# Seven block products in place of eight in a down projection on one core

## The chip, the cores and the metric

The kernel runs on one NeuronCore of a Trainium2 chip. The core has five engines with instruction queues of their own: TensorE (PE in the profile; its weight loads are shown apart as PEld), VectorE (DVE), ScalarE (ACT), GpSimd (POOL) and SyncE (SP, which only issues transfers here). The metric is the device time of one execution in microseconds (us); lower is better. PSUM, which TensorE writes its products to, has eight banks; one bank holds a tile of 128 x 512 float32.

## The reference

One layer of a post-norm encoder on a sequence of 512 tokens and 1024 channels: a token mixer of three branches, then a gated MLP with a causal convolution. Only the MLP's end matters here. With `h` (512 x 1024) after the second modulation and `c` the condition:

```python
def _conv_ffn(h, w_up, conv_w, conv_b, w_down):
    z = h @ w_up                                # 512 x 5632
    ...                                         # three-tap causal convolution along the sequence
    val, gate = jnp.split(zc, 2, axis=-1)
    return (jax.nn.silu(gate) * val) @ w_down   # 512 x 2816 times 2816 x 1024

    y = _conv_ffn(h, w_up[l], conv_w[l], conv_b[l], w_down[l])
    x = _layer_norm(ALPHA * x + gt_f[:, None, :] * y) * ln_f_g[l] + ln_f_b[l]
```

`gt_f` is a row of 1024 gates, a matrix product of `silu(c)` with a slice of `w_ada`, plus a bias.

## The kernel before, in words

Every large product is computed in three matmuls: an operand is split into a high part (rounded to the fast matmul type) and a low part (the remainder), and high x low, low x high and high x high are added up in one PSUM bank. The split of a weight tile is a cast on ScalarE (high) and a subtraction on VectorE (low).

The layer runs as one straight program; TensorE goes from one product to the next: input projections and attention, the pooling branch and its merge, the gating branch (`uv_half`, `gated`) and the other two merges, an output projection (`project_out` with name "o"), the up projection, and the down projection (`project_out` with name "d").

A framework orders the instructions of each engine beforehand from the program's dependencies: where a step of higher rank (earlier in the program) isn't ready, a later one that is ready can be put ahead of it. `behind_split(work)` puts a piece of side work behind the latest subtraction of a weight split on the same engine. Tiles of one tag share a fixed number of buffers: `raw` (128 x 1024, three; weights as loaded), `whi` and `wlo` (two each; split weights of the moment), `act` (48 of 128 x 512), `h` (16), `pt` (8), `pad` (5). A load on SP waits until a buffer of its tag is free, and what is queued behind it on SP waits with it.

**Up projection** (the loop `for i in range(NP)`, NP = 22). A turn makes two 128-row blocks of `z` (one of the values, one of the gates, 24 matmuls each), the convolution (L1410, L1413, L1417), the SiLU (L1427) and the product on GpSimd (L1428). The result, channels x tokens, is split into `f{i}h` and `f{i}l` (L1431, L1432). On every second turn up to the 16th it also loads and adds up one piece of `w_ada` for the gates (`ada_piece`); after the last of them `ada_rows` sums over partitions with four matmuls against ones (`pgt`, L871) and leaves the gate row, broadcast to 128 partitions, in `gtfb`.

**Down projection** (L1124 to L1158, then `mm3` at L107 to L109). It has 22 chunks k of 128 rows of `w_down`. Each chunk is loaded (512 KB), **multiplied by the gate row on GpSimd** (L1124, two halves), split, and multiplied with the four token tiles t and two column halves n: 4 x 2 x 3 matmuls of 512 columns into eight banks, which are all in use from the first chunk to the last. The first 18 chunks pass through `whi`/`wlo`; the last four are split into resident tiles of tag `h` (L1134, L1135), so that the last products can be ordered by output: all four chunks of one (t, n), then the next. After each t, `finish` adds the residual straight from PSUM (L1448), takes the statistics (L1455, L1457), and normalises and stores the 128 rows: two centrings on VectorE (L1462), one half scaled on VectorE (L1474), the other on ScalarE (L1471) and GpSimd (L1472). The last half of the last tile is computed in two products of 256 columns, so that its statistics come sooner (L1454).

## Time and profile before

| | before |
|---|---|
| median of three runs | 953.91 us (953.81 to 954.74) |
| profiled execution, own time | 953.8 us |
| its span, first to last instruction | 952.1 us |
| outside the span | 1.7 us |
| granted TensorE clock | 0.998 |

The profile's page gives the busy time of each engine, the span in 40 slices, the transfer queues, the chain of work that ended last, and the costliest groups of instructions. Other views of the trace give that chain or all instructions in order of time, groups of instructions by line and shape, busy times by stretch, and the instructions around one tile. Durations are in us; "mean ns of one" in nanoseconds; "idle before, releaser" is how long the engine stood still ahead of an instruction and who ended that.

### The profile page before, as it was taken

The numbers are of one execution on the slowest core, as the hardware profiler recorded it, in microseconds if no ns is written. First come the engines' busy times: TensorE is split into PE (matmuls) and PEld (weight loads), VectorE is DVE, ScalarE is ACT, GpSimd is POOL, SyncE is SP. The second block draws the span as 40 slices with busy tenths as digits, with TensorE's granted clock in tenths as the row PEclk, the third lists the DMA queues.
The fourth block names the chain that finished last, engine by engine and source line by source line (L and its number), as shares of the span: only waits on it lengthen the run. The fifth ranks groups of instructions, "written<-read, shape, count | busy, mean of one in ns | idle before, by whom it ended". The sixth has DMA issues, their size and how long they took to land.

```text
span 952.1 us, 12075 instructions
## 1 busy us (share of the span) xinstructions
PE 938.9 (99%) x4524; PEld 792.6 (83%) x4524; DVE 594.2 (62%) x860; ACT 380.5 (40%) x623; POOL 290.7 (31%) x258
## 2 busy tenths in 40 slices
PE   7999999999999999999999999999999999999996
PEld 6988888888888888888888889988888888888885
DVE  7966668546686575667244589575655665733268
ACT  4576555533334322233322434654444444321121
POOL 4741121122350032303053713021111121756653
PEclk9999999999999999999999999999999999999999
DMA  9823212144436533554244440233343342432222
GB/s 323 323 64 109 59 34 83 45 133 154 133 100 215 194 112 121 177 190 154 90 134 131 156 155 24 68 126 117 112 135 129 116 127 90 127 116 89 97 81 88
DMA packets 46458, 119.77 MB, mean 126 GB/s; under 512 B 5792, under 2 KB 9280, under 8 KB 46400
## 3 DMA queue, kind: packets, MB, share of 16 engines
q1 hardware_dynamic: 45648, 118.39, 38.0%
q8 instruction: 35, 0.57, 0.2%
q10 hardware_dynamic: 432, 0.55, 0.2%
q14 instruction: 23, 0.19, 0.1%
q0 software_dynamic: 320, 0.07, 0.0%
HBM read 116.86 MB, written 2.13 MB: 125 GB/s over the span
## 4 chain that ended last, share of the span: by engine, by line
PE 97%; DVE 1%; DMA 0%; POOL 0%; issue 0%; ACT 0%; POOLq 0%; SPq 0%; ACTq 0%
PE pzu L117 7%; PE pzu L114 7%; PE pzu L115 7%; PE py L115 5%; PE py L114 5%; PE py L117 5%; PE pg L114 4%; PE pg L115 4%; PE pg L117 4%; PE pyd L1158 3%; PE pyd L1155 3%; PE pyd L1157 3%; PE lat L527 2%; PE pu L114 2%; PE pu L115 2%; PE pu L995 2%
## 5 line engine op out<-in xcount | busy, mean ns | idle before, releaser
L94 DVE TENSOR_TENSOR wupl<-wup,wuph 128x1024 fp32r<-128x1024 f32 x38 | 48.6, 1280 | 71.9 <-PE pzu L117 45.9
L1124 POOL TENSOR_TENSOR d<-d,gtfb 128x512 f32<-128x512 f32 x44 | 75.5, 1738 | 34.1 <-DMA d<-in_wdn 34.1
L1428 POOL TENSOR_TENSOR zc<-zc 128x512 f32<-128x512 f32 x22 | 29.7, 1351 | 174.8 <-ACT zc L1427 154.0
L1129 DVE TENSOR_TENSOR dl<-d,dh 128x1024 fp32r<-128x1024 f32 x18 | 28.2, 1569 | 56.2 <-PE pyd L1155 52.1
L93 ACT CAST wuph<-wup 128x1024 fp32r<-128x1024 f32 x38 | 39.9, 1050 | 46.8 <-PE pzu L115 46.8
L93 ACT CAST wbh<-wb 128x1024 fp32r<-128x1024 f32 x24 | 25.3, 1054 | 69.2 <-PE py L115 50.4
L418 POOL TENSOR_TENSOR mg<-mg,th 128x512 f32<-128x512 f32 x16 | 31.3, 1955 | 68.4 <-DVE th L415 68.4
L853 DVE SCALAR_TENSOR_TENSOR ada<-adar,cact,ada 128x512 f32<-128x512 f32 x56 | 49.1, 907 | 2.0 <-DMA adar<-in_ada 2.0
L94 DVE TENSOR_TENSOR wgl<-wg,wgh 128x1024 fp32r<-128x1024 f32 x22 | 28.3, 1285 | 30.7 <-ACT wgh L93 16.3
L1128 ACT CAST dh<-d 128x1024 fp32r<-128x1024 f32 x18 | 18.9, 1052 | 60.8 <-PE pyd L1158 36.9
L1410 ACT ACTIVATE zc<-pzu,cols 128x512 f32<-128x512 f32 x44 | 34.2, 779 | 21.8 <-PE pzu L117 17.4
L94 DVE TENSOR_TENSOR wbl<-wb,wbh 128x1024 fp32r<-128x1024 f32 x24 | 30.9, 1286 | 14.9 <-ACT wbh L93 6.5
L772 POOL TENSOR_SCALAR pe<-pe,mx 128x128 f32<-128x128 f32 (+3 forms) x32 | 17.0, 534 | 69.3 <-DVE mx L771 43.2
L1413 DVE SCALAR_TENSOR_TENSOR zc<-pzu,cols,zc 128x511 f32<-128x511 f32 x44 | 32.6, 743 | 4.2 <-ACT zc L1410 4.2
L93 ACT CAST wgh<-wg 128x1024 fp32r<-128x1024 f32 x22 | 23.3, 1059 | 29.2 <-PE pg L115 23.4
L1417 DVE SCALAR_TENSOR_TENSOR zc<-pzu,cols,zc 128x510 f32<-128x510 f32 x44 | 32.6, 744 | 0.8
L1427 ACT ACTIVATE zc<-zc 128x512 f32<-128x512 f32 x22 | 13.9, 631 | 42.2 <-DVE zc L1417 42.1
L926 POOL TENSOR_TENSOR asum<-apad 128x527 f32<-128x527 f32 x8 | 12.3, 1544 | 54.9 <-ACT apad L921 28.0
L297 DVE SCALAR_TENSOR_TENSOR acc<-ada,cact,acc 128x256 f32<-128x256 f32 (+1 forms) x29 | 27.7, 954 | 1.7 <-DMA ada<-in_ada1p 0.7
L415 DVE SCALAR_TENSOR_TENSOR th<-th,py 128x512 f32<-128x512 f32 x16 | 11.0, 686 | 26.8 <-PE py L117 26.8
L1102 POOL TENSOR_TENSOR oraw<-oraw,gttb 128x512 f32<-128x512 f32 x6 | 11.1, 1864 | 43.1 <-DMA oraw<-in_wo 43.1
L1124 POOL TENSOR_TENSOR o<-o,gttb 128x512 f32<-128x512 f32 x10 | 17.8, 1798 | 12.4 <-DMA o<-in_wo 11.3
(1480 smaller groups left out, 3093.8 us busy)
## 6 DMA issues: line engine op xcount, KB each, us to landing
wup<-in_wup SPq DMA_DIRECT2D x44, 512.0 KB, 3.4
adar<-in_ada SPq DMA_DIRECT2D x64, 256.0 KB, 3.8
wb<-in_wb SPq DMA_DIRECT2D x24, 512.0 KB, 3.5
wg<-in_wg SPq DMA_DIRECT2D x22, 512.0 KB, 3.5
d<-in_wdn SPq DMA_DIRECT2D x22, 512.0 KB, 3.5
ada<-in_ada1p SPq DMA_DIRECT2D x24, 256.0 KB, 5.1
wa<-in_wa SPq DMA_DIRECT2D x8, 512.0 KB, 3.5
wsg<-in_wsg SPq DMA_DIRECT2D x8, 512.0 KB, 3.5
```

The lines of the kernel that those rows point to most:

```text
L93: nc.scalar.copy(out=hi[:, :n], in_=raw[:, :n])
L94: ins = nc.vector.tensor_tensor(out=lo[:, :n], in0=raw[:, :n], in1=f(hi[:, :n]), op=ALU.subtract)
L114: nc.tensor.matmul(o, wh[:, c], xl[k], start=k == 0, stop=False)
L115: nc.tensor.matmul(o, wh[:, c], xh[k], start=False, stop=False)
L117: nc.tensor.matmul(o, wl[:, c], xh[k], start=False, stop=k == KT - 1)
L418: nc.gpsimd.tensor_tensor(out=merged[m], in0=merged[m], in1=th, op=ALU.add)
L853: nc.vector.scalar_tensor_tensor(out=acc[n], in0=src, scalar=cact[:, k : k + 1], in1=acc[n], op0=ALU.mult, op1=ALU.add,)
L1124: nc.gpsimd.tensor_tensor(out=halves[n], in0=halves[n], in1=gt[n], op=ALU.mult)
L1410: nc.scalar.activation(t, pz, AF.Identity, bias=cols[:, cc + 3 : cc + 4], scale=cols[:, cc + 2 : cc + 3])
L1413: nc.vector.scalar_tensor_tensor(out=t[:, 1:512], in0=pz[:, 0:511], scalar=cols[:, cc + 1 : cc + 2], in1=t[:, 1:512], op0=ALU.mult, op1=AL ...
L1417: nc.vector.scalar_tensor_tensor(out=t[:, 2:512], in0=pz[:, 0:510], scalar=cols[:, cc : cc + 1], in1=t[:, 2:512], op0=ALU.mult, op1=ALU.add,)
L1428: nc.gpsimd.tensor_tensor(out=val, in0=val, in1=gate, op=ALU.mult)
```

## The change

Write two consecutive chunks (2p and 2p+1) of the activations as the two halves of the inner dimension, the tokens as two halves of 256, and the columns as two halves of 512. A 2 x 2 block product then takes seven block products in place of eight (the Winograd form: four sums of weight blocks, four sums of activation blocks, and seven sums of products). There are HP = 11 such pairs p.

- **Weight sums.** `combine_weights(p)` loads the four 128 x 512 blocks of a pair, makes four block differences and sums on VectorE, and stores four blocks to scratch in DRAM with transfers issued by GpSimd. Two of the eleven are put behind steps of the gating branch's `v1`, four behind the odd steps of the second merge, five behind the first five steps of the third.
- **Activation sums.** In the up projection's loop, `first_left` and `other_lefts` replace the split of `val`: four sums of 128 x 256 on VectorE, and seven split operands for each pair in seven `act` tiles of 128 x 512 (high and low, 256 tokens each). Four of the seven tiles stay for the first sweep; three are stored to scratch by GpSimd.
- **Two sweeps.** Seven products x two token tiles are 14 banks, so that they are computed in two sweeps: first products 1, 5, 6, 7 (eight banks), then 2, 3, 4 (six banks). In the first sweep each pair needs two raw buffers (512 KB each), and `reload(p)` brings the pair's three stored activation tiles back, with transfers issued by GpSimd into `act` tiles that the first sweep has freed. The last R1 = 2 pairs of the first sweep and R2 = 5 of the second use resident tiles and are ordered by output.
- **Between the sweeps** VectorE and ScalarE empty the eight banks, form the common sums, and add them, times the gates, to `x1` (the residual). GpSimd no longer multiplies weights by gates; it multiplies six output tiles.
- **End.** `take` multiplies a product by the gate row, adds it to `x1` or subtracts it, and takes the statistics: three VectorE instructions where `finish` had two. `row_end` is the rest of `finish`.
- **Gate row.** `ada_piece(3, ..)` (tag `pt`, every second turn) becomes `ada_wide_piece` (tag `act`, turns 3 to 10); `ada_rows` becomes `ada_parts` (no matmul) and `ada_bounced_rows`, two trips through DRAM.

```diff
+    def combine_weights(p):
+        b = []
+        for k in (2 * p, 2 * p + 1):
+            for n in range(2):
+                blk = act_t(f"wb{k}{n}", F32)
+                nc.sync.dma_start(
+                    out=blk, in_=A["wdn"][k * P : (k + 1) * P, n * 512 : (n + 1) * 512]
+                )
+                b.append(blk)
+        b11, b12, b21, b22 = b
+        for dst, x, y, op in (
+            (b22, b22, b12, ALU.subtract), (b12, b12, b11, ALU.subtract),
+            (b11, b22, b11, ALU.add), (b21, b11, b21, ALU.subtract),
+        ):
+            ins = nc.vector.tensor_tensor(out=dst, in0=x, in1=y, op=op)
+        for dst, src in (
+            (t3_t[p], b22), (wide_t[p][:, 512:], b12), (wide_t[p][:, :512], b11), (t4_t[p], b21),
+        ):
+            nc.gpsimd.dma_start(out=dst, in_=src)
...
+    def split256(dst, src):
+        nc.scalar.copy(out=dst[:, :256], in_=src)
+        nc.vector.tensor_tensor(out=dst[:, 256:], in0=src, in1=f(dst[:, :256]), op=ALU.subtract)
...
+    def other_lefts(p, v1, v2):
+        for dst, x, y, op in (
+            (e[:, :256], v1[:, 256:], v2[:, 256:], ALU.add),
+            (d[:, :256], e[:, :256], v1[:, :256], ALU.subtract),
+            (d[:, 256:512], v1[:, :256], v1[:, 256:], ALU.subtract),
+            (e[:, 256:512], v2[:, :256], d[:, :256], ALU.subtract),
+        ):
+            nc.vector.tensor_tensor(out=dst, in0=x, in1=y, op=op)
...
+        for dst, src in zip(spill[p], (yh, yl, ys)):
+            nc.gpsimd.dma_start(out=dst, in_=f(src))
...
-        ah = act_t(f"f{i}h")
-        al = act_t(f"f{i}l")
-        nc.scalar.copy(out=ah, in_=val)
-        nc.vector.tensor_tensor(out=al, in0=val, in1=f(ah), op=ALU.subtract)
+        if i % 2 == 0:
+            first_left(i // 2, val)
+            held[0] = val
+        else:
+            other_lefts(i // 2, held[0], val)
...
+    def sweep_step(p, chunks):
+        for (wh, wl), users in chunks:
+            for rest in range(2):
+                for t in range(2):
+                    for acc, (xh, xl), c in users:
+                        ts_ = slice(t * P, (t + 1) * P)
+                        if rest:
+                            nc.tensor.matmul(acc[t], xh[:, ts_], wl[:, c], start=False, stop=False)
+                        else:
+                            nc.tensor.matmul(acc[t], xh[:, ts_], wh[:, c], start=p == 0, stop=False)
+                            nc.tensor.matmul(acc[t], xl[:, ts_], wh[:, c], start=False, stop=False)
...
+    for p in range(HP - R1):
+        rb, ra = raws1(p)
+        wb_ = split_wide(rb, D, "db")
+        wa_ = split_wide(ra, D, "da")
+        x = lefts1(p)
+        sweep_step(p, (
+            (wb_, ((m1, x[1], lo_half), (m7, x[7], hi_half))),
+            (wa_, ((m6, x[6], lo_half), (m5, x[5], hi_half))),
+        ))
+        reload(p)
...
+    for p in range(HP - R2):
+        rc, rd = raws2(p)
+        wc_ = split_wide(rc, D, "dc")
+        wd_ = split_wide(rd, 512, "dd")
+        x = lefts2(p)
+        sweep_step(p, (
+            (wc_, ((m2, x[2], lo_half), (m3, x[3], hi_half))),
+            (wd_, ((m4, x[4], lo_half),)),
+        ))
...
+    def take(t, n, acc, op, slot, c=slice(0, 512)):
+        q = pt_t("fq")
+        w = c.stop - c.start
+        nc.vector.tensor_tensor(out=q[:, :w], in0=acc, in1=gt_f[n][:, c], op=ALU.mult)
+        ins = nc.vector.tensor_tensor(out=x1[t][n][:, c], in0=x1[t][n][:, c], in1=q[:, :w], op=op)
+        if slot is not None:
+            ins = nc.vector.bn_stats(out=stats[t][:, slot, :], in_=x1[t][n][:, c])
...
+    for t in range(2):
+        close(2, m2[t], t)
+        take(t, 0, m2[t], ALU.add, 0)
+        close(3, m3[t], t)
+        take(t, 1, m3[t], ALU.add, 1)
+        row_end(t, 2)
+        if t == 0:
+            close(4, m4[0], 0)
+            take(2, 0, m4[0], ALU.subtract, 1)
+            row_end(2, 2)
+    close(4, m4[1][:, :256], 1, halves[0])
+    extra = ps("pe4x")
+    close(4, extra[:, :256], 1, halves[1], True)
...
+    row_end(3, 4)
```

`close(c, acc, t)` runs the three matmuls of each of the last five pairs into `acc`.

More of the change, by code (lines that the diff above doesn't have):

```diff
@@ L38 @@
 C_CONV = 59
-N_COLS = C_CONV + 4 * 2 * NP
+C_GTF = C_CONV + 4 * 2 * NP
+N_COLS = C_GTF + 8
 K_FREQ = 0
@@ L1396, in trunk @@
+    held = [None]
     for i in range(NP):
@@ L1437, in trunk @@
+    ws1 = {}
+    for p in range(HP - R1, HP):
+        rb, ra = raws1(p)
+        (w1, w7), (w6, w5) = (
+            split_narrow(r, 2, f"d{c}{p}", h_t) for c, r in (("b", rb), ("a", ra))
+        )
+        ws1[p] = {1: w1, 7: w7, 6: w6, 5: w5}
     lnfg = row_tiles(4, act_t, "lnfg")
     lnfb = row_tiles(5, act_t, "lnfb")
-    def finish(t, py):
-        dst = [pt_t(f"out{t}{n}") for n in range(2)]
-        wide = 256 if t == TT - 1 else 512
-        st = sm.tile([P, 4, 6], F32, name="std", tag="std", bufs=2)
-        for n in range(2):
-            with ExitStack() as order:
-                if n and t == TT - 1:
-                    order.enter_context(tc.issue_after(ins.ins))
+    stats = [sm.tile([P, 4, 6], F32, name=f"std{t}", tag=f"std{t}", bufs=1) for t in range(TT)]
```

200 lines of the change are left out of this document (182 added, 18 removed).

## The prediction

> **What bounds the kernel now.** The page first: its busy times and the chain that ended last.
>
> ```profile
> span 952.1 us, 12075 instructions
> ...
> PE 938.9 (99%) x4524; PEld 792.6 (83%) x4524; DVE 594.2 (62%) x860; ACT 380.5 (40%) x623; POOL 290.7 (31%) x258
> ...
> PE 97%; DVE 1%; DMA 0%; POOL 0%; issue 0%; ACT 0%; POOLq 0%; SPq 0%; ACTq 0%
> ```
>
> TensorE is the chain; VectorE has over a third of the span free. So fewer matmuls are worth their time, as long as nothing else becomes late in the same place. The chain in order of time gives the price of a matmul, and the timeline the two ends of the down projection:
>
> ```profile
> 767.61 1.82 PE pzu L117 x8
> 769.43 0.92 PE pgt L871 x4
> ...
> 915.45 1.81 PE pyd L1155 x8
> ...
> 920.89 1.81 PE pyd L1155 x8
> ```
>
> ```profile
> 824.62 0.39 PE L1157 MATMUL pyd<-dh,f0h 128*128 128x512 f32 x1
> ...
> 940.51 0.21 DVE L1457 BATCH_NORM_AGGREGATE mv<-std 128x2 f32<-128x12 f32 x1
> 940.75 0.15 DVE L1459 TENSOR_SCALAR rs<-mv 128x1 f32<-128x1 f32 x1
> 940.82 1.41 DVE L1462 SCALAR_TENSOR_TENSOR out<-out,mv,lnfg 128x512 f32<-128x512 f32 x2
> ...
> 942.74 0.74 DVE L1474 SCALAR_TENSOR_TENSOR out<-out,rs,lnfb 128x512 f32<-128x512 f32 x1
> ...
> 944.21 0.28 PE L108 MATMUL pye<-d21h,f21l 128*128 128x256 f32 x1
> 944.33 0.28 PE L109 MATMUL pye<-d21h,f21h 128*128 128x256 f32 x1
> ...
> 945.12 0.40 DVE L1454 TENSOR_TENSOR out<-out,pye 128x256 f32<-128x256 f32 x1
> 945.55 0.43 DVE L1455 BATCH_NORM_STATS2 std<-out 128x6 f32<-128x256 f32 x1
> ```
>
> Two chunks end 5.44 us apart, and a chunk has 24 matmuls: 0.2267 us each; a half-width one takes 0.12 (944.21 to 944.33). TensorE ends at 944.33 + 0.12 = 944.45, the last statistics at 945.55 + 0.43 = 945.98, 1.53 later. What follows (normalising, the last store) stays as it is, so I sum up to the last statistics.
>
> **TensorE: 15.84 saved.** Before, 22 x 8 x 3 = 528 matmuls; after, 11 pairs x 7 products x 2 token tiles x 3 = 462. The 66 are worth 14.96. The four of the gate row go: 0.92. Thirty half-width matmuls stand for 15, before 24 for 12: 0.04 more. The down projection then starts at 823.70 and, unhindered, TensorE ends at 823.70 + 447 x 0.2267 + 30 x 0.12 = 928.6.
>
> **The tail: 10.9 given back.** The costs of the other engines, from the groups by line and the transfers:
>
> ```profile
> L94 DVE TENSOR_TENSOR wupl<-wup,wuph 128x1024 fp32r<-128x1024 f32 x38 | 48.6, 1280 | 71.9 <-PE pzu L117 45.9
> ...
> L1455 DVE BATCH_NORM_STATS2 std<-out 128x6 f32<-128x512 f32 x6 | 4.1, 692 | 0.1
> ...
> L1432 DVE TENSOR_TENSOR f20l<-zc,f20h 128x512 fp32r<-128x512 f32 x1 | 1.8, 1775 | 0.0
> L872 DVE TENSOR_TENSOR gtfb<-pgt,gtfb 128x512 f32<-128x512 f32 x2 | 1.4, 679 | 0.0
> ...
> L1432 DVE TENSOR_TENSOR f18l<-zc,f18h 128x512 fp32r<-128x512 f32 x1 | 0.7, 687 | 0.0
> ```
>
> ```profile
> L1134 ACT CAST d18h<-d x2: 622/624/626, 907.5 to 909.7; 128x512 fp32r<-128x512 f32 x2
> ```
>
> ```profile
> d<-in_wdn SPq DMA_DIRECT2D x22, 512.0 KB, 3.5
> ...
> x<-in_x SPq DMA_DIRECT2D x14, 256.0 KB, 2.7
> ```
>
> The last closing before, among the busy times by stretch (the columns are named further down; GpSimd's is the 7.38):
>
> ```profile
> 922.30:944.50 22.20, 22.20 (x110) 18.78 (x108) 17.84 (x33) 2.80 (x4) 7.38 (x7) 1.00 0.13 50
> ```
>
> A half-row instruction of VectorE takes 0.68 to 0.69, and with 0.03 between two (945.12 + 0.40 to 945.55) 0.72. A `take` is three: 2.15. A `row_end` is 940.51 to 942.23 plus 0.74, 2.4 with some overlap. The last operations (three on `m4[1]`, three on the extra bank) make 3.2. After the first product of the closing, VectorE owes five takes, three row ends, one last split and these: 10.75 + 7.2 + 0.72 + 3.2 = 21.9, without a pause. The closing itself (25 groups of three full and 30 half matmuls) is 20.6 of TensorE, from 908.0.
>
> When does that first product end? It needs weights of all five resident pairs, and these come through three raw buffers. A 512 KB buffer turns in 3.5 (landing) + 0.62 (first cast) + 2 x 0.72 = 5.6; a 256 KB one in 2.7 + 0.62 + 0.72 = 4.0; so a pair every 9.6 / 3 = 3.2. A step of the sweep lasts 18 x 0.2267 = 4.08, so the step p=5 starts at 903.9. In the sweep a raw buffer is freed when TensorE has released a low buffer: the first resident load is issued 0.7 after p=4 starts, lands near 904.0, and the fifth 4 x 3.2 later, near 917. First cast and low half make it 918.1, its product 919.1. Then 21.9: VectorE is done at 941.0, whatever order TensorE takes meanwhile. That is 12.4 after TensorE against 1.53: 10.9 more. If the loads were hidden, VectorE would follow TensorE's closing and finish near 934.1: 4.0 more (below nothing isn't possible, it has a third instruction for each product). If GpSimd's row ends slowed every SBUF subtraction to the 1.775 of the row above, up to 18; GpSimd was busy in the last closing for 7.38 of 22.2, so I stop at 14. [...]
>
> **Between the sweeps: 1.5.** VectorE has 12 instructions to empty the banks, six gated additions and three statistics (about 14.5), and four resident splits (2.9): 17.4, in TensorE's 16 x 0.68 = 10.9 of that closing. Of the 6.5 that are left, the last three additions (3.0) can come later; the second sweep's first low half (1.28) is queued behind the rest, and TensorE waits for it after 12 matmuls (2.7): 17.4 - 3.0 + 1.28 - 10.9 - 2.7 = 2.1. Splits put into gaps would make it 0; I take 1.5, nearer the sum.
>
> **First sweep: 0.7.** Each pair loads 2 x 0.524 MB of weights and reloads 0.786 MB in 5.44. That is 337 GB/s; what the transfer engines can do is seen at the start:
>
> ```profile
> core 0: us, PE busy (x) PEld busy (x) DVE busy (x) ACT busy (x) POOL busy (x), PEclk, DMA share, GB/s
> 0.00:30.00 30.00, 24.66 (x133) 21.63 (x134) 23.27 (x39) 15.80 (x30) 12.93 (x24) 1.00 0.94 336
> 324.00:341.00 17.00, 17.00 (x76) 14.08 (x76) 10.72 (x15) 5.12 (x7) 0.00 (x0) 1.00 0.62 198
> 341.00:401.00 60.00, 60.00 (x266) 49.67 (x266) 38.07 (x46) 13.40 (x14) 21.28 (x14) 1.00 0.37 121
> 473.00:522.00 49.00, 49.00 (x218) 40.58 (x217) 20.99 (x24) 14.28 (x17) 18.24 (x14) 1.00 0.40 128
> 622.00:769.00 147.00, 147.00 (x650) 121.74 (x649) 90.44 (x112) 66.47 (x85) 22.91 (x17) 1.00 0.37 122
> ```
>
> Full demand meets full supply, softened by three buffers loaded ahead: 0.7 for unevenness, between 0 and the second rival's 7.2. VectorE needs 2 x 1.28 of each 5.44 here.
>
> **Nothing, with its cover.** GpSimd's 44 gate multiplications go, but they fed weights in time. The activation sums cost VectorE some 2.8 more for each pair; in 622 to 769 that is 19 on top of 90.4 of 147. The weight sums are 44 subtractions of 0.72 (32): 5.8 on 10.72 of 17, 11.5 on 38 of 60, 14.4 on 21 of 49. They wait in VectorE's queue for their own loads, and the next split's low half is queued behind them, TensorE behind that; the cover is that weights are split nearly two chunks (10.9) ahead. The combines move 2.1 MB each: 4.2 into 324 to 341, where 5.7 is the ceiling and 3.4 is there, the rest drains into the next stretch; 10.5 + 6.3 = 16.8 into 473 to 522 against 16.5. On SP each combine puts four loads ahead of weights. If the cover is gone, some 5 us.
>
> **Sum.** -15.84 + 10.9 + 1.5 + 0.7 = -2.7. The profiled execution's 953.8 becomes 951.1 (a span near 949.4). The median of the runs lies 0.1 above that execution: 951.2.
>
> **Rivals.** *The tail is hidden* (faster). Resident weights come early enough, and the closing is paced by TensorE: 4.0 in place of 10.9, 944.3. For it: loads land faster than 3.2 a pair if the order ahead of them frees a buffer sooner. Against it: three buffers, and the row of 3.5. Chance 0.21.
>
> *The reloads take half of the transfers* (slower). Where both the weights' queue and GpSimd's have work, each gets half, 168 GB/s; a pair's 1.049 MB then takes 6.24 in place of 5.44, in nine pairs 7.2 in place of 0.7: 957.6. It decides once the weights get under 193 GB/s. For it: the demand above, and no row shows a large transfer issued by GpSimd. Against it: the reloads pause when no buffer is free. [...] Chance 0.17.
>
> *The weight sums lose their cover* at 324 to 341 or 473 to 522: 5 us, 956. For it: transfers at the ceiling twice. Against: the two chunks ahead. Chance 0.08.
>
> That fewer matmuls run than counted isn't in question: 4524 - 66 - 4 + 3 = 4457 should be on the page.
>
> **Numbers.** The forecast's case has 0.54, and by its bounds (tail 8 to 14, transition 0 to 2) runs from 947.5 to 955; its centre is 0.9 beyond 0.2% (1.9 us, about what a measurement can tell from no change), so I give 0.30 of it to faster, 0.15 to the same, 0.09 to slower. Faster: 0.30 + 0.21 = 0.51; same 0.15; slower 0.09 + 0.17 + 0.08 = 0.34. The range reaches from the hidden tail (943) to the shared transfers (959).
>
> **What would show it.** Right: VectorE without a pause over the last 22 us, TensorE done some 12 before the last statistics; 5.44 a pair in the first sweep with transfers near 0.94; no idle TensorE before 820. Wrong: the last statistics within 6 of TensorE's end (first rival); steps over 6 in the first sweep, ended by DMA (second); idle TensorE in 324 to 401 or 473 to 540 (third). A TensorE that idles over 3 at the change of sweeps, or a slower split on VectorE beside GpSimd's transfers, would be a cost that I have not priced.

## The result, and the profile after

The changed kernel takes 968.36 us (median of four runs, 966.76 to 972.45) against 953.86 of the kernel before on the same chip: 1.0157 times as long, interval 1.0144 to 1.0171. That is slower by 14.5 us; the forecast was 951.2, faster, with a range up to 959. The profiled execution of the changed kernel took 972.45 itself, with a span of 970.7, 18.6 more than the span before; the sums below are made against that span, so they explain 18.6 and not the 14.5 of the medians.

From the page of the changed kernel, the span, the busy times, the transfers and the chain by engine:

```profile
span 970.7 us, 12642 instructions
...
PE 931.5 (96%) x4457; PEld 780.5 (80%) x4457; DVE 684.8 (71%) x1035; ACT 410.2 (42%) x683; POOL 279.7 (29%) x333
...
DMA packets 69663, 168.89 MB, mean 174 GB/s; under 512 B 9968, under 2 KB 13472, under 8 KB 69600
...
PE 81%; DMA 8%; DVE 6%; ACT 2%; issue 2%; POOL 1%; SPq 0%; POOLq 0%; ACTq 0%; DVEq 0%
```

TensorE has the 4457 matmuls that were counted, and yet carries only 81% of the chain, where it had 97%: transfers, VectorE and ScalarE now end 16% of it. Where, the timeline of the changed kernel shows (the first matmul of each sweep, the last resident low half, the first `take`, the last matmul, the last statistics):

```profile
830.02 0.39 PE L1573 MATMUL pd<-dbh,xa 128*128 128x512 f32 x1
...
897.83 0.39 PE L1573 MATMUL pe<-dch,z 128*128 128x512 f32 x1
...
943.27 0.69 DVE L1557 TENSOR_TENSOR dd10l<-dd,dd10h 128x512 fp32r<-128x512 f32 x1 [0.56 <-ACT dd10h L1556]
943.88 1.28 DVE L1697 TENSOR_TENSOR fq<-pe,gtf 128x512 f32<-128x512 f32 x2
...
948.54 0.28 PE L110 MATMUL pe4x<-dd10h,z 128*128 128x256 f32 x1
...
963.08 0.25 DVE L1706 BATCH_NORM_AGGREGATE mv<-std 128x2 f32<-128x24 f32 x1
```

The up projection's first matmul with a wide weight tile, 616.9 before, stands at 623.3 (the groups by line): 6.4 lost by then. From there to the down projection 1.0 is saved (the gate row's matmuls). The down projection on TensorE lasts from 830.02 to 948.82: 118.8 against 120.0 before, where the matmul count gives 104.9; 13.9 are lost inside it, 8.0 from 830.02 to 897.83 (264 matmuls, 59.8) and 5.9 from there. The tail, from the last matmul's end to the end of the last aggregation, is 14.5 against 1.7. The rest is 1.6 longer. 6.4 - 1.0 - 1.2 + 12.8 + 1.6 = 18.6.

The busy times by stretch, first of the kernel before, then of the changed one (columns as in the prediction: length, busy time with count of PE, PEld, DVE, ACT, POOL, clock, DMA share, GB/s):

```profile
506.00:560.00 54.00, 54.00 (x240) 44.71 (x239) 31.62 (x39) 19.63 (x31) 24.92 (x15) 1.00 0.47 153
830.00:880.00 50.00, 50.00 (x222) 41.39 (x222) 15.29 (x11) 11.15 (x11) 31.34 (x20) 1.00 0.37 115
```

```profile
506.00:560.00 54.00, 50.25 (x214) 40.90 (x213) 34.77 (x41) 17.32 (x26) 27.56 (x23) 0.97 0.66 228
830.00:880.00 50.00, 46.11 (x196) 36.00 (x195) 23.71 (x26) 18.67 (x21) 20.30 (x36) 1.00 0.98 330
```

In both stretches TensorE ran without a pause before, and stands still now; in the second the transfers take 0.98 of the engines' time. The chain of the changed kernel in order of time names the releasers there, and the list of its PE waits their length:

```profile
512.72 2.47 DMA wt<-wb
515.19 8.62 DMA wb<-in_wdn
...
533.06 1.15 DVE wbl L95
534.22 3.39 DMA o<-in_wo
...
856.41 6.61 DMA db<-wt
...
865.45 6.96 DMA da<-wt
...
875.22 10.25 DMA db<-wt
```

```profile
PE pd L1573 <- ACT dbh L1546: 3.3, 2, 2.6
PE pyo L108 <- DVE o2l L1168: 2.9, 1, 2.9
PE pe L1571 <- DVE dcl L1547: 2.3, 2, 1.3
PE pe L1573 <- ACT ddh L1546: 1.0, 1, 1.0
PE py L118 <- DVE wbl L95: 0.9, 1, 0.9
```

The first two chain rows belong to weight sums of the third merge: the store of one to scratch, and the load of a block for the next, which takes 8.62; what is queued behind it ends in TensorE's waits on `wbl` (0.9) and `o2l` (2.9). The last three are weights of the first sweep that land after 6.6 to 10.3 us; without the reloads (e1 below) such loads land in 3.0 and 3.8.

### The profile page after: what moved, and what is told of

Same layout as the page of the kernel before. It is cut to its first block, busy times and chain, and to the rows that moved or that the text cites. A ratio compares the mean times of both kernels' runs of the same rounds, so it can differ in the third digit from the quotient of the medians.

```text
span 970.7 us, 12642 instructions
## 1 busy us (share of the span) xinstructions
PE 931.5 (96%) x4457; PEld 780.5 (80%) x4457; DVE 684.8 (71%) x1035; ACT 410.2 (42%) x683; POOL 279.7 (29%) x333
## 4 chain that ended last, share of the span: by engine, by line
PE 81%; DMA 8%; DVE 6%; ACT 2%; issue 2%; POOL 1%; SPq 0%; POOLq 0%; ACTq 0%; DVEq 0%
PE pzu L115 7%; PE pzu L118 7%; PE pzu L116 7%; PE pg L115 4%; PE pg L116 4%; PE pg L118 4%; PE py L115 4%; PE py L118 4%; PE py L116 4%; DMA db<-wt 3%; PE lat L528 2%; PE pu L115 2%; PE pa L115 1%; PE pu L116 1%; PE pu L1021 1%
## 5 line engine op out<-in xcount | busy, mean ns | idle before, releaser
L95 DVE TENSOR_TENSOR wupl<-wup,wuph 128x1024 fp32r<-128x1024 f32 x38 | 53.6, 1410 | 23.6 <-PE pzu L118 18.2
L1524 POOL TENSOR_TENSOR zc<-zc 128x512 f32<-128x512 f32 x22 | 30.1, 1370 | 125.4 <-ACT zc L1523 102.1
L975 POOL DMA_DIRECT2D wt<-wb x44 | 24.5, 557 | 96.2 <-DVE wb L971 91.6
L971 DVE TENSOR_TENSOR wb<-wb,wb 128x512 f32<-128x512 f32 x44 | 39.6, 901 | 10.7 <-DMA wb<-in_wdn 10.1
L854 DVE SCALAR_TENSOR_TENSOR ada<-adar,cact,ada 128x512 f32<-128x512 f32 x42 | 38.8, 961 | 2.3 <-DMA adar<-in_ada 2.3
L1588 POOL DMA_DIRECT2D z<-ys x33 | 17.5, 539 | 25.6 <-PE pd L1571 9.4
L1547 DVE TENSOR_TENSOR dbl<-db,dbh 128x1024 fp32r<-128x1024 f32 x9 | 11.0, 1225 | 18.8 <-ACT dbh L1546 14.4
L1523 ACT ACTIVATE zc<-zc 128x512 f32<-128x512 f32 x22 | 13.9, 631 | 22.4 <-DVE zc L1511 22.4
L1547 DVE TENSOR_TENSOR dal<-da,dah 128x1024 fp32r<-128x1024 f32 x9 | 11.0, 1224 | 14.6 <-ACT dah L1546 12.1
```

The costliest lines, as they stand in the source:

```text
L95: ins = nc.vector.tensor_tensor(out=lo[:, :n], in0=raw[:, :n], in1=f(hi[:, :n]), op=ALU.subtract)
L854: nc.vector.scalar_tensor_tensor(out=acc[n], in0=src, scalar=cact[:, k : k + 1], in1=acc[n], op0=ALU.mult, op1=ALU.add,)
L971: ins = nc.vector.tensor_tensor(out=dst, in0=x, in1=y, op=op)
L1524: nc.gpsimd.tensor_tensor(out=val, in0=val, in1=gate, op=ALU.mult)
```

## The experiments

Four theories for four places: the weight sums (merge), the reloads (first sweep), VectorE's queue (change of sweeps), VectorE's work behind the last resident weights (tail). Each expectation names a rival of its own; the one that most of the later runs share is that one resource, VectorE or the transfers, is full from the up projection on, so that a repair in one place only moves the wait to the next. The table puts every profile in the same marks, read from its timeline and groups as above. *Merge* is the time of the up projection's first wide matmul; *down* and *tail* are as above; their sum is what the down projection costs. The ratio is that of the median times to the kernel before on the same chip. The marks are those of one execution each, and small differences between them tell nothing: the changed kernel and e4 have the same instructions in the same order up to the last products, and their first sweeps differ by 1.5 (67.8 and 66.3).

| kernel | merge | down | tail | sum | median us | ratio (interval) |
|---|---|---|---|---|---|---|
| before | 616.9 | 120.0 | 1.7 | 121.7 | 953.9 | 1 |
| changed | 623.3 | 118.8 | 14.5 | 133.3 | 968.4 | 1.0157 (1.0144 to 1.0171) |
| e1 no reload | 622.4 | 110.3 | 14.3 | 124.5 | 967.9 | 1.0144 (1.0123 to 1.0165) |
| e2 sums earlier | 616.8 | 117.7 | 14.3 | 132.0 | 965.4 | 1.0117 (1.0102 to 1.0132) |
| e3 more load room | 617.9 | 119.9 | 8.4 | 128.3 | 966.3 | 1.0135 (1.0116 to 1.0154) |
| e4 no gate | 622.2 | 117.3 | 12.4 | 129.7 | 966.4 | 1.0131 (1.0115 to 1.0146) |
| e5 reloads spread | 618.0 | 118.8 | 14.3 | 133.0 | 968.3 | 1.0142 (1.0127 to 1.0157) |
| e6 three together | 617.8 | 119.4 | 6.9 | 126.3 | 960.1 | 1.0058 (1.0042 to 1.0075) |
| e7 GpSimd low halves | 617.2 | 118.7 | 6.7 | 125.4 | 960.0 | 1.0061 (1.0046 to 1.0076) |
| e8 residents early | 616.9 | 122.3 | 7.1 | 129.4 | 963.4 | 1.0093 (1.0078 to 1.0108) |
| e9 reloads paced | 619.3 | 121.3 | 14.6 | 135.9 | 972.1 | 1.0189 (1.0172 to 1.0206) |
| e10 paced and repairs | 616.8 | 120.0 | 6.9 | 126.9 | 960.6 | 1.0064 (1.0047 to 1.0080) |
| e11 six residents | 617.0 | 120.6 | 6.9 | 127.5 | 961.7 | 1.0075 (1.0060 to 1.0090) |
| e12 reloads held | 619.9 | 116.4 | 14.3 | 130.7 | 966.3 | 1.0125 (1.0110 to 1.0140) |
| e13 held and repairs | 618.4 | 117.1 | 10.0 | 127.1 | 960.6 | 1.0064 (1.0047 to 1.0080) |
| e14 sums later | 617.3 | 111.9 | 10.1 | 122.0 | 955.2 | 1.0007 (0.9998 to 1.0017) |
| e15 row ends off | 617.3 | 112.2 | 10.2 | 122.4 | 955.0 | 1.0012 (1.0003 to 1.0021) |
| e16 sums later alone | 621.7 | 114.8 | 15.2 | 130.0 | 967.6 | 1.0133 (1.0116 to 1.0150) |
| e17 residents between | 616.8 | 113.2 | 4.8 | 118.0 | 952.3 | 0.9981 (0.9972 to 0.9989) |
| e18 fewer late reloads | 618.0 | 114.0 | 4.8 | 118.8 | 952.9 | 0.9988 (0.9977 to 1.0000) |

**The reloads left out.** The second sweep takes the first sweep's tiles as operands, so it computes on other data.

```diff
-        ts = [act_t(f"z{i}{p}") for i in range(3)]
-        for dst, src in zip(ts, spill[p]):
-            nc.gpsimd.dma_start(out=dst, in_=src)
-        left2.append(ts)
+        left2.append([left1[p][2], left1[p][3], left1[p][1]])
```

> The second sweep takes three of the first sweep's activation tiles in place of the stored ones, so that the 33 reloads (8.7 MB, issued by GpSimd) are left out; the stores to scratch stay, and the second sweep's products are of other data. Theory (reloads and weights together ask for more than the transfer engines move, and the weights land late): the first sweep's pairs return to 5.44 us each, weights land in under 5 us, its 7.8 us of loss go, the program takes 959 to 962. Rival (the three raw buffers, two to a pair, turn too slowly whatever else is moved): weights still land late or TensorE still waits over 5 us in the first sweep, and the time stays within 2 us of 968.

Its busy times by stretch, and its weight loads (KB each, median us to landing) behind those of the changed kernel:

```profile
830.00:880.00 50.00, 50.00 (x222) 41.40 (x221) 28.80 (x33) 23.18 (x30) 3.33 (x4) 1.00 0.74 235
```

```profile
z<-ys POOLq DMA_DIRECT2D x33, 256.0 KB, 9.0
da<-wt SPq DMA_DIRECT2D x11, 512.0 KB, 6.3
...
db<-wt SPq DMA_DIRECT2D x11, 256.0 KB, 6.6
```

```profile
da<-wt SPq DMA_DIRECT2D x11, 512.0 KB, 3.8
...
db<-wt SPq DMA_DIRECT2D x11, 256.0 KB, 3.0
```

TensorE has no pause in the first sweep, and the weights land in 3.8 and 3.0, where the changed kernel has 6.3 and 6.6 (and 9.0 for the reloads, `z<-ys`). TensorE's part is 8.5 shorter. So the reloads cause the first sweep's loss. The time, however, hardly fell (967.9, where the theory said 959 to 962): in this profile the span goes on for 8.0 us after the issue of the last store, 2.5 in the changed kernel, with no work in it; the store itself had landed at 960.0, 6.5 before the end. What these 5.5 are stays open; the marks up to the statistics are what this run is used for.

**The weight sums elsewhere.** Five of them move from the third merge to the gating branch's steps 1 to 5.

```diff
         behind_split(ada_piece, 2, g)
+        if 1 <= g < 6:
+            behind_split(combine_weights, 5 + g)
...
-        if m < 5:
-            behind_split(combine_weights, 6 + m)
```

> The five weight sums beside the third merge go to five steps of the stage before it (the gated products), one for each step; nothing is left out. Theory (in the third merge their transfers and their place ahead of the output projection's loads make these late): TensorE's stand-still between 506 and 627 goes, the up projection starts some 6 us earlier, the program takes 961 to 963. Rival (the sums' work on VectorE has no room anywhere): the stand-still moves to the gated products and the time stays within 2 us of 968.

```profile
506.00:560.00 54.00, 54.00 (x240) 44.71 (x239) 32.08 (x40) 19.46 (x31) 25.18 (x15) 1.00 0.45 147
```

Its busy times: TensorE is full again in 506 to 560, and the merge mark is back at 616.8, with no new wait where the sums went. The time falls by 3, not by 6.4, and the other rows of the table show why: with the sums left in place the mark lies anywhere from 617.9 to 623.3, in e5 at 618.0 although its instructions up to the down projection are those of the changed kernel, in the same order on every engine. The stall is one of timing, from 1 to 6.4; the changed kernel's profiled execution has the full one, and it is also 4.1 above the median of its runs. With the sums moved (e2, e6 to e8, e10, e11, e13 to e15, e17, e18) it lies between 616.8 and 618.4.

What differs is how long two sums took on VectorE behind the late load, first in the changed kernel, then in e5:

```profile
527.06 5.40 DVE L971 TENSOR_TENSOR wb<-wb,wb 128x512 f32<-128x512 f32 x2
```

```profile
523.60 2.38 DVE L971 TENSOR_TENSOR wb<-wb,wb 128x512 f32<-128x512 f32 x2
```

Two of them take 1.4 elsewhere. In the changed kernel GpSimd multiplies `o` at that time (525.2 to 528.3 and 529.4 to 531.9), and the sums have `wbl` queued behind them. In the four kernels where both sums were slow, 1.66 to 3.60 each (changed, e1, e4, e16), the mark lies at 621.7 to 623.3; in the four where only the second was, at 1.66 or 1.67 (e3, e5, e9, e12), at 617.9 to 619.9. So the late load and VectorE's slow sums beside GpSimd go together in this stall; no run separates them.

**More raw buffers for the second sweep.** Its half-wide weights go to `act` tiles; three raw buffers then serve the full ones alone.

```diff
-            raw_pair(((lo_half, t4_t[p]),), "dd"),
+            small_raw(t4_t[p], f"ddr{p}"),
```

> In the second sweep the half-wide weights are loaded into tiles of the activations' tag in place of raw buffers, so that the three raw buffers serve the wide ones alone; nothing is left out. Theory (the resident weights of the second sweep come late because three raw buffers turn once in 3.2 us a pair, and VectorE's work piles up behind them): the last wide weights land 4 to 5 us earlier against TensorE's first closing product, the second sweep's waits shrink, and 4 to 8 us go: 960 to 964. Rival (VectorE's own work in the last closing sets the end, whenever weights come): the gap between TensorE's end and the last statistics stays at 13 to 15 us and the time falls by less than 2.

The tail falls from 14.5 to 8.4, the sum by 5.0: the resident low halves are done by 933.1, and VectorE then works without a pause. The tail hangs on when the resident weights arrive. The median falls by 2.0 only, where the theory said 4 to 8; the profiled execution, 963.0, is the fastest of its four.

**The gate multiplication left out** of the last products (the output is that of an ungated sum there):

```diff
-        nc.vector.tensor_tensor(out=q[:, :w], in0=acc, in1=gt_f[n][:, c], op=ALU.mult)
-        ins = nc.vector.tensor_tensor(out=x1[t][n][:, c], in0=x1[t][n][:, c], in1=q[:, :w], op=op)
+        ins = nc.vector.tensor_tensor(out=x1[t][n][:, c], in0=x1[t][n][:, c], in1=acc, op=op)
```

> In the last closing the multiplication of products by the gate row is left out in six of seven places (VectorE adds the product straight from PSUM), so that the output is of other values. Theory (after the resident weights VectorE runs without a pause to the end, so that every instruction of it counts): 6 x 0.72 us less, the end comes 4 to 5 us earlier, 963 to 965. Rival (the end waits for late weights or transfers): under 1.5 us.

The sum falls by 3.6, but 1.5 of that lie in the first sweep, which the edit doesn't touch. From the second sweep's first matmul to the end of the span it is 69.4 in place of 72.9: 3.5, six instructions of 0.6. So both the start of VectorE's last work and its amount count.

**Reloads spread, then paced: two tests that did not test.** One reload at every second step and the rest in the closing (e5); then, ahead of each, a one-column copy by GpSimd that waits for the step's weights (e9).

```diff
-        reload(p)
+        if p in (1, 3, 5, 7):
+            reload(len(left2))
...
+    for _ in range(4):
+        reload(len(left2))
```

```diff
+        pace = sm.tile([P, 1], F32, name="pace", tag="pace")
+        nc.gpsimd.tensor_copy(out=pace, in_=f(after[:, :1]))
```

> The same bytes as the changed kernel, but the reloads spread: one pair after the first sweep's steps 1, 3, 5 and 7, four pairs while it closes, three in the second sweep's first steps. Theory (a step of 5.44 us with a reload asks for as much as the transfers give, about 335 GB/s, so whatever is put there in addition stretches it): two steps with one reload ask for 264 GB/s, the first sweep's steps come back to about 49 us for nine from 49.8 plus the waits behind them, 7 us of the 7.8 go, and the time is about 961 us. Rival (the total of the transfers is what binds, about 29 MB in 105 us, wherever they stand): the wait moves to the closing and to the second sweep's steps, and the time stays within 2 us of 968.

> The run with spread reloads did not spread them: GpSimd issued each as soon as its tiles were free (seven at 833 us, then one every 1.4 us), whatever its place in the program. Here GpSimd copies one column of a split weight before each reload, so that it waits for the step; one reload at steps 1, 3, 5 and 7, four beside the splits of the first sweep's residents, three in the second sweep. Nothing else differs from the changed kernel. Theory (only the reloads beside the streamed steps cost time): the first sweep's transfers fall from 330 to about 270 GB/s, its nine steps are back within 1 us of 49, and the time from the first down projection matmul to the last statistics is 5 to 8 us shorter than the 133 of the changed kernel; about 962 us. Rival (the total of the transfers binds, wherever they stand): the waits move on and this length stays above 131.

GpSimd's timeline in e9:

```profile
834.72 3.74 POOL L1590 DMA_DIRECT2D z<-ys  x7
...
849.37 0.53 POOL L1590 DMA_DIRECT2D z<-ys  x1 [0.81 <-DMA ys<-yl]
849.89 0.20 POOL L1587 COPY pace<-dah 128x1 f32<-128x1 f32 x1
```

Seven reloads are issued together at 834.7, and fourteen stand before the copy of step 3, which should have let only three pass: nothing but free tiles and stored data hold a reload, and the order of the queue is made beforehand from dependencies, so a place in the program holds nothing. The transfers ran at 354 and 345 GB/s in 830 to 880. Neither theory was touched; the sums are 133.0 and 135.9.

**Three repairs at once, and two more ideas.** e6 has the sums moved, the half-wide raws in `pad` tiles (as e3 in `act`), and the spread reloads of e5; e7 makes five resident low halves on GpSimd; e8 instead splits two resident pairs in the first sweep (the edits of e7 and of e8):

```diff
-            nc.vector.tensor_tensor(out=lo, in0=raw[:, c], in1=f(hi), op=ALU.subtract)
+            (eng or nc.vector).tensor_tensor(out=lo, in0=raw[:, c], in1=f(hi), op=ALU.subtract)
```

```diff
+        if p in (2, 5):
+            resident2(HP - R2 + (p == 5), h_t)
```

> The weight sums moved to the gated steps, the reloads spread, and the second sweep's half-wide weights read into five buffers of their own, so that two raws of three no longer serve both. Theory (the losses lie in separate places and add up): 6.4 of the third merge, some 6 to 7 of the first sweep, about 5 of the second sweep and the end are saved, 968.4 less 18 is about 951 us, near the kernel before or 2 to 3 us below it, and the time from the last matmul to the last statistics is about 8. Rival (one resource, VectorE or the transfers, is full from the up projection on, and each repair only moves the wait): 958 us or more, with the tail back at 12 to 14.

> The kernel with the three repairs, with the five low halves of the half-wide resident weights made by GpSimd instead of VectorE (five subtractions of 128x512 of about 0.7 us fewer on VectorE in the last 25 us). Theory (the end is VectorE's own count of work): the tail is 3 to 4 us shorter and so is the time. Rival (VectorE's operations stretch beside GpSimd's, 0.69 to 1.6 and more as seen beside its gate multiplications): the gain is below 1 us, or it is a loss.

> The kernel with the three repairs, with two of the second sweep's five resident pairs read and split already after the first sweep's steps 2 and 5, and the first sweep's residents in the tiles that these free; two reloads fewer while the first sweep closes, two more in the second sweep. Theory (the end is VectorE's count of work behind the last streamed step, and it has 2.8 us free in each of the first sweep's steps): six subtractions of about 0.67 fewer there, the tail is about 4 us shorter, the time 3 to 4 us below the kernel with the three repairs. Rival (the transfers of the first sweep are filled up again, 305 of 335 GB/s): its steps stretch by 2 to 4 us, which takes the gain back.

e6 gains 8.2 of the median: the merge and the tail, as theory had it, but the first sweep nothing, since the reloads were not spread. e7 is the same within its interval: GpSimd takes 1.36 to 2.15 for each low half that took VectorE 0.69, and the last one is done 106.1 after the first matmul, 105.1 in e6. e8 loses 3.2 against e6: its sweeps wait more (122.3) for a tail that is no shorter.

> All repairs at once: the weight sums moved, the half-wide raws in buffers of their own, five resident low halves by GpSimd, the reloads paced. Theory: against the kernel with GpSimd low halves (960.0) another 5 to 7 us go in the first sweep: 953 to 955, the same as the kernel before within 0.2%. Rival (transfers bind in total): 959 or more.

> The same with six resident pairs in the second sweep's closing instead of five: 18 more matmuls (4.1 us) run behind the last streamed step, against 2.0 us more of splits there. Theory (the tail is what VectorE has left over the closing): the tail is 1 to 2 us shorter, 952 to 954. Rival (the loads and splits of the residents come late, so the closing itself waits): 1 to 3 us longer than with five.

These two (e7 with the copies of e9; `R2 = 6`) tell of pacing as little as e9 does; a sixth resident pair leaves the tail at 6.9.

**The reloads really held.** GpSimd writes one column of the tile itself from the step's split weight; the reload overwrites it and cannot start before. One reload follows each second step, as in e9, and the others come later (e12; e13 is the same on top of e7's repairs).

```diff
         for dst, src in zip(ts, spill[p]):
+            nc.gpsimd.tensor_copy(out=dst[:, :1], in_=f(after[:, :1]))
             nc.gpsimd.dma_start(out=dst, in_=src)
```

> Neither of the two runs that meant to spread the reloads did so: their issues stood in the queue one every 1.4 us as before, ahead of the copies that were to hold them. Here GpSimd writes one column of each tile from the step's split weight before the reload overwrites it, so that the transfer cannot begin before. One reload at steps 1, 3, 5 and 7, four beside the residents of the first sweep, three in the second sweep; nothing else differs from the changed kernel. Theory (only what is asked for beside the streamed steps costs time): 840 to 870 falls from 390 to about 270 GB/s, the nine steps come to 49 to 50 us, and the length from the first down projection matmul to the last matmul falls from 118.7 to 112-114; about 962 us. Rival (the total binds wherever it stands): that length stays above 117.5.

> The kernel with the weight sums moved, the half-wide raws in their own buffers and the five low halves by GpSimd, with the reloads held in the same way. Theory: the length from the first down projection matmul to the last falls from about 118.4 to 112-113, the time from 960.0 to 954-956, the same as the kernel before within 0.2%. Rival: 959 or more, since the reloads come to stand before the second sweep's steps.

Busy times and the timeline of TensorE and VectorE in e12:

```profile
830.00:880.00 50.00, 50.00 (x222) 41.40 (x221) 26.45 (x30) 21.04 (x26) 23.20 (x43) 1.00 0.86 280
890.00:910.00 20.00, 14.02 (x46) 9.84 (x47) 17.71 (x21) 4.29 (x5) 13.48 (x19) 0.83 0.81 263
```

```profile
891.37 3.08 DVE L1646 SCALAR_TENSOR_TENSOR x<-x,uq 128x512 f32<-128x512 f32 x1
...
896.36 1.91 DVE L1547 TENSOR_TENSOR dcl<-dc,dch 128x1024 fp32r<-128x1024 f32 x1
898.19 1.77 DVE L1625 SCALAR_TENSOR_TENSOR x<-x,u 128x512 f32<-128x512 f32 x1
...
898.32 1.21 PE L1571 MATMUL pe<-dcl,z 128*128 128x512 f32 x4 [2.80 <-DVE dcl L1547]
901.68 1.22 PE L1571 MATMUL pe<-ddl,z 128*128 128x512 f32 x2 [2.15 <-DVE ddl L1547]
```

The first sweep now runs full at 280 GB/s, with all reloads kept, some of them later: the total of the transfers does not bind, their crowding does. But of the 8.0 gained there 5.5 are lost again from the second sweep's first matmul on (56.5 in place of 51.0; down 116.4, between what the theory and the rival gave): 46 matmuls in 890 to 910, where 88 fit. TensorE waits for `dcl` and `ddl`, and these stand in VectorE's queue behind the gated additions, one of which takes 3.08 and one 1.77 while GpSimd multiplies. In e13 the rival's number, 960.6, came true for this reason, and for another: TensorE's part is 2.9 shorter than in e10, and the tail 3.1 longer (10.0).

**The gated additions later, on VectorE alone.** Each of the six is queued behind one streamed step's low half, its multiplication no longer on GpSimd: e14 on top of e13, e16 on the changed kernel alone; e15 is e14 with a part of two row ends moved to ScalarE and GpSimd.

```diff
-        nc.gpsimd.tensor_tensor(out=u, in0=u, in1=gt_f[n], op=ALU.mult)
+        nc.vector.tensor_tensor(out=u, in0=u, in1=gt_f[n], op=ALU.mult)
...
+        with tc.issue_after(getattr(last_split[0], "ins", last_split[0])):
+            add_gated(*waiting.pop(0))
```

```diff
-        for n, a, b, eng in ((1, 0, 512, nc.vector), (0, cut, 512, nc.gpsimd), (0, 0, cut, nc.vector)):
+        for n, a, b, eng in ((1, 0, 512, nc.gpsimd if t in (0, 2) else nc.vector), (0, cut, 512, nc.gpsimd), (0, 0, cut, nc.vector)):
```

> The kernel with all repairs and held reloads (960.6), with the six gated additions of the first sweep's sums taken out of the change of sweeps: each (multiplication and addition, both on VectorE, none on GpSimd) is queued behind the low half of one streamed step of the second sweep. Theory (what e12 and e13 lost at the change of sweeps, PE 14 of 20 us in 890 to 910, is VectorE's queue, its operations stretched beside GpSimd's): the two waits of 3.2 and 2.2 go, and the length from the first down projection matmul to the last falls from 117 to 111-112; 955 to 957. Rival (the transfers, 280 to 390 GB/s in 880 to 910, make the second sweep's weights late): the waits stay, now ended by transfers or by ScalarE's halves, and the length stays above 115.5.

> The same, and in the row ends of rows 0 and 2 the last step of the second column half on ScalarE and GpSimd, as the first half has it already (two operations fewer on VectorE in the last 20 us). Theory (the end is VectorE's count): 1.5 to 2.5 us below the kernel before it. Rival (VectorE's operations stretch beside the added GpSimd work): within 1 us of it.

> The changed kernel with only the six gated additions moved into the second sweep's steps and to VectorE. Theory: the second sweep's length to the last matmul falls from 50.9 by about 3 to 5 us, but the end keeps VectorE's added 8 us of multiplications in the steps, so the resident splits may come later and the tail stay at 14; 964 to 967. Rival (GpSimd's multiplications did not matter): 967 to 970.

VectorE in e14, the same instructions as in e12:

```profile
891.91 0.69 DVE L1656 SCALAR_TENSOR_TENSOR x<-x,uq 128x512 f32<-128x512 f32 x1
...
893.12 0.68 DVE L1635 SCALAR_TENSOR_TENSOR x<-x,u 128x512 f32<-128x512 f32 x1
...
894.91 1.22 DVE L1555 TENSOR_TENSOR dcl<-dc,dch 128x1024 fp32r<-128x1024 f32 x1
```

The instructions are back at 0.68 and 1.22, the down projection loses 5.3 more of its waits (111.9), and the time is 955.2, level with the kernel before, though transfers ran at 348 GB/s in 890 to 910: VectorE's queue was the cause there, not the transfers. The edit moves the additions and takes the multiplications off GpSimd at once; which of the two did more is not separated. Alone (e16) it shortens TensorE's part by 4.0 as well, but the tail grows by 0.7 and the median falls by 0.8 only, within the intervals. e15 gives nothing, as its rival had it (tail 10.2).

**Resident weights between the streamed steps.** In e14 the last resident pair's low half comes at 924.3, and every accumulator of the closing needs that pair. e17 loads and splits three of the five pairs between the steps (first edit); e18 also moves two reloads into the first sweep (second edit).

```diff
+        if 2 <= p < 5:
+            resident2(HP - R2 + p - 2)
```

```diff
-        if p in (1, 3, 5, 7):
+        if p in (1, 2, 4, 5, 7, 8):
```

> The kernel with all repairs and the additions later (955.2), with three of the second sweep's five resident pairs read and split between its streamed steps 3 to 5 instead of behind them. In that kernel the low half of the last resident pair is done at 924.3, TensorE's last matmul follows at 935.9 and VectorE works without a gap from 927.9 to the last statistics at 945.8, with 5 us idle just before. Theory (every accumulator of the closing waits for the last pair, so the end starts with that split): the last split comes 2 to 4 us earlier, the tail shrinks by as much, 951.5 to 953.5, at or just below the kernel before. Rival (VectorE and the transfers are full in the streamed steps, 8.3 to 10 of 10 us and 305 to 390 GB/s): the streamed steps wait instead, 955 or more.

> The same, with two of the reloads moved from the change of sweeps into the first sweep (after steps 1, 2, 4, 5, 7 and 8), where 264 GB/s become about 290. Theory (only the sum within each stretch counts, and the first sweep has room up to about 335): the second sweep's first weights come sooner, 1 to 2 us below the run beside it. Rival (two reloads close together make single loads late, as the 1.4 us wait left in the first sweep shows): within 1 us of it or above.

VectorE's and TensorE's timeline in e17:

```profile
919.65 1.13 DVE L1567 TENSOR_TENSOR dc10l<-dc,dc10h 128x512 fp32r<-128x512 f32 x1
...
922.78 0.69 DVE L1715 TENSOR_TENSOR fq<-pe,gtf 128x512 f32<-128x512 f32 x1 [2.00 <-PE pe L110]
...
936.53 0.28 PE L110 MATMUL pe4x<-dd10h,z 128*128 128x256 f32 x1
...
941.36 0.26 DVE L1724 BATCH_NORM_AGGREGATE mv<-std 128x2 f32<-128x24 f32 x1
```

The last low half of a wide resident tile is done at 920.8, 3.5 earlier; the tail is 4.8, and the time 952.25, 1.8 below the kernel before (0.9981, interval 0.9972 to 0.9989). It is the one version here that beats both, the kernel before by 0.2% on one chip. TensorE's part is 1.4 longer than in e14; one wait of 3.15 for a low half that GpSimd makes (`dd6l`) lies in it. e18's marks are within 1.2 of it, as the rival had it.

## Why the prediction was wrong

**TensorE, 15.84 saved: right.** 4457 matmuls, 0.2267 apart where nothing waits (222 in 50 us in e1), and 1.0 for the gate row.

**"Nothing, with its cover": the first step that failed.** The weight sums were costed at nothing, with some 5 us if the cover was gone. It went at the end of the second of the two stretches that I had named by their transfers (324 to 341, 473 to 522); in the first nothing was lost. The third rival, given 0.08, was right in kind: the chain leaves TensorE at 509, the late load lies at 515 to 524, and TensorE's two waits follow between 533 and 550, with slower matmuls behind them (clock 0.97 in 506 to 560). But I had summed rates by stretch; what fails is one load of 8.62 in VectorE's queue and, behind it, two sums of 1.77 and 3.60 beside GpSimd's multiplications, where I had counted 0.72. 6.4 in this profile, 1 to 6.4 over the kernels that left the sums in place.

**"First sweep: 0.7": failed in size, by the second rival's mechanism.** The rival said 7.2; 8.0 were lost up to the change of sweeps. The reloads land after 9.0 us and slow the weights from 3.8 to 6.3 (`da`), and without them the loss is gone (e1). I had named 336 GB/s, seen at the start, as what the engines can do, and priced full demand at 0.7. The transfers of the changed kernel from 842 to 886, where both queues are busy (q0 is GpSimd's, q1 SyncE's: packets, MB, share of time):

```profile
DMA packets 8163, 16.94 MB, mean 385 GB/s; under 512 B 923, under 2 KB 923, under 8 KB 8161
...
q0 software_dynamic: 4835, 9.04, 63.1%
q1 hardware_dynamic: 3326, 7.87, 50.8%
```

The engines moved 385, more than I had allowed, and yet the weights got 179 of it (7.87 MB in 44 us) and the reloads with the last stores 205: the weights are under the 193 at which the rival was to decide. At 179 a pair's 1.049 MB takes 5.9, which is 3.8 more over nine pairs; the rest of the 8.0 lies in single late loads and in matmuls at a slower clock behind the waits (0.96 in 842 to 886), so that 7.2 comes so near is in part luck. That each of two queues gets half was an assumption of the forecast; measured here were the two shares, 179 and 205, which are near even, and `da` landing after 6.3 beside reloads and 3.8 without.

**"Between the sweeps: 1.5": failed in size.** I counted instructions at 0.68. The queue was right, the price was not: in the changed kernel additions beside GpSimd's multiplications took up to 1.78 and a low half 1.71 in place of 1.22; 5.9 were lost in the second sweep, of which 3.7 are waits (2.3 for `dcl`, 1.0 for `ddh`, 0.4 for `us`). With the additions moved (e16) 2.2 are lost there. The prediction had named a slower split beside GpSimd's transfers as a cost not priced; what the changed kernel shows is that low half, slow beside GpSimd's multiplications. It had the row of 1.775 and used it for the tail only.

**"The tail: 10.9": right in kind, 2 too small.** VectorE works without a pause from 943.3 to the last statistics, and the work is near the count (19.5 from the first `take` in place of 21.9). But the resident weights came later against TensorE than worked out: TensorE ended 4.9 after that first `take`, not 9.5. That the tail shrinks if the loads come earlier (first rival) is what e3 and e17 show: 8.4 and 4.8.

**The combination: why the sign was wrong.** The rivals were given chances as if one at most came true. They lie in different places and add up. With the rivals' own prices the sum was -2.7 + 6.5 + 5 = +8.8; with what the second sweep and the tail lost beyond their terms (4.4 and 1.9) and the 1.6 by which the end, taken as unchanged, grew, it is 16.7, between the 14.5 of the medians and the 18.6 of the profiled execution. The range ended at 959 because it took one rival at a time.

Left open: whether e17's remaining losses (8.3 of 113.2 in TensorE's part) can go, and e1's last 5.5 us.

## What to carry to other kernels

When a change loads several engines at once, price each place where its work lands and add the mishaps up before taking chances: four losses came together here, of 5.9 to 12.8 us in the profile (the last foreseen at 10.9), against a gain of 15.84. A repair in one place can uncover the next (e12, e13), so look at the marks and not at the time alone. A place in the program did not delay a transfer on the second queue (e9 issued seven reloads together at 834.7); a dependency of its own, a write to its tile, did (e12 issued three at 837.5 and the next three at 844.9). Where all last products need the last resident weights, the tail starts when these are split, so split them between the streamed steps (tail 10.1 in e14, 4.8 in e17).

## What the runs showed of the hardware

**VectorE beside GpSimd.** The instruction `x<-x,u`, both inputs in SBUF, took 0.68 in e14, without GpSimd's multiplications, and 1.77 in e12 beside them, 3.08 for `x<-x,uq`; `us<-pd,us`, with an input in PSUM, stayed at 0.68 in the same stretch. GpSimd's own instructions were longer there too: e12 has VectorE's `dcl` from 896.36 to 898.27 (1.91, 1.22 in e14), GpSimd's `uc` from 897.15 to 899.41 (2.26, 1.30 for the `uc` at 891.34), VectorE's `x<-x,u` from 898.19 to 899.96 and GpSimd's `us` from 899.37 to 901.08, each ending 0.6 to 1.1 after the one before it.

**The clock after a pause.** After the wait of 2.88 in the changed kernel's third merge, TensorE's matmuls start 0.43 apart in place of 0.23; the granted clock of 550 to 553 was 0.50:

```profile
550.12 0.79 PE L108 MATMUL pyo<-o2l,mgh 128*128 128x512 f32 x1 [2.88 <-DVE o2l L1168]
...
551.14 0.63 PE L110 MATMUL pyo<-o2h,mgh 128*128 128x512 f32 x1
551.57 0.63 PE L108 MATMUL pyo<-o2l,mgh 128*128 128x512 f32 x1
```

In e12 the same follows the two waits of 2.80 and 2.15 (clock 0.83 in 890 to 910): the 5 us of waiting cost, as an estimate, some 1.6 more in slow matmuls (eight at 0.43 in place of 0.23). Not every pause had it: some 2 us after 2.65 in the changed kernel (up to 879.31) and after 3.01 in e1 (up to 898.94) the matmuls were 0.43 apart, after 3.15 in e17 (up to 902.69) they stayed at 0.23. In the changed kernel's tail, where TensorE has nothing left to do after 948.8, the granted clock of 945 to 970 was 0.65.
